# Seven products per pair of d_ff blocks in the gate and up projections of a decoder trunk, with down products between them

## Chip, cores and metric

One NeuronCore of a Trainium2 chip runs the kernel. The metric is device time in microseconds (us); each time is that of one execution, and a kernel's time is the median of its executions. Engines are named as in the profile: PE is TensorE (PEld its weight loads), DVE is VectorE, ACT is ScalarE, POOL is GpSimd, SP issues most of the DMAs. PSUM is the memory that PE accumulates into, in banks; the other engines drain it.

## What is computed

One layer of a decoder for 512 prompt tokens and 8 single-token samples (520 token columns in all), d_model 1024, d_ff 2816, in float32: a mixer of three branches, then the feed-forward sub-layer, then a norm. The change lies in the feed-forward part alone:

```python
def conv_ffn(h, lp, prev):
    a = h @ lp['w_ffn_gate']
    up = h @ lp['w_ffn_up']
    ...
    c = lp['conv_b'] + sum(w[j] * ext[:, j:j + T] for j in range(CONV_W))
    y = (jax.nn.gelu(c) * up) @ lp['w_ffn_down']
    return y, ext[:, T:]
```

`x += conv_ffn(rmsnorm(x))` follows the mixer, and a last `rmsnorm` gives the output.

## The kernel before, in words

**Layout and precision.** Activations stand transposed: 128 channels on the partitions, 520 token columns on the free axis, worked on in two halves of 260 (`NH`, `H`). d_model is 8 blocks of 128 (`KB`), d_ff is 22 (`NFF`). Each operand of a product is kept as two fp32r tiles, a rounded "hi" and the remainder "lo", and `mm3` (L426) issues three matmuls for each pair of 128x128 weight block and 260 columns: hi by hi, hi by lo, lo by hi.

**Weights.** `UNITS` (L56 to L79) is the list of weight units in the order of use; each is up to 8 blocks, 512 KB. `w_load` fetches a unit on SP's queue into a tile `wraw`; `w_split` (L335) makes `whi` (ACT copy) and `wlo` (DVE subtract) of all its 1024 columns. `begin` (L431) and `ahead` (L441) load and split one to two units ahead of use. `product` (L449) issues a unit's matmuls into one of two PSUM tiles `mm` of two banks each, one bank for each token half: 8 blocks x 2 halves x 3 = 48 matmuls. A smaller PSUM tile is called `SD`.

**Order.** The body (L257) is one Python program; DVE, ACT and POOL work that is not tied to a product is kept in generators ("lanes", L230), and `pump` (L394) and `drain` (L408) put their operations between others by a table of modelled costs (`Clock`, L85) at build time. Each engine then runs its own list in order. All operations are recorded by a helper, so the profile gives them line L226.

**Feed-forward part.** For each of 22 d_ff blocks (`for ob in range(NFF)`) a gate unit `fg` and an up unit `fu` are multiplied. The gate product is drained by DVE (times `rs2`), goes through the three-tap convolution (two column copies on POOL, one `Identity` on ACT, two scalar_tensor_tensor on DVE, an add and two copies on POOL), `gelu` on ACT, times `rstd` and times the up product on DVE; ACT's copy and DVE's subtract make the hi and lo tile of hidden block `hid(ob, ·)`. Only then come the down products: for each of 8 output blocks m, 22 hidden blocks in units of 8, 8 and 6, 132 matmuls, one DVE add onto x (`B<-mm,B`). The last output is made in two token halves (`PIECES`, `last`), and `finish` (final norm: two matmuls of `ones` into `SD`, Ln and Exp on ACT, DVE and POOL products, stores) of the first half runs beside the products of the second:

```python
    for c0, n in PIECES:
        for j, _ in enumerate(last(c0, n)):
            if todo and j in (0, 5, 6, 7):
                next(todo, None)
```

Of the kernel before, what the change touches and what calls it, by code (L numbers as in the profile page):

```python
# [15 lines left out]
P = 128  # L16
# [39 lines left out]
def stream_units():  # L56
# [6 lines left out]
    for i in range(NFF):  # L63
        u += [("fg", i), ("fu", i)]
    for i in range(8):
        u += [("dn", (i, 0)), ("dn", (i, 1)), ("dn", (i, 2))]
# [6 lines left out]
def unit_blocks(u):  # L73
    return 6 if u[0] == "dn" and u[1][1] == 2 else 8
# [4 lines left out]
for _u in UNITS:  # L79
    UNIT_OFF.append(_o)  # L80
    _o += P * P * unit_blocks(_u)
N_W = _o


class Clock:  # L85
# [4 lines left out]
    LAT = 0.13  # L90

# [68 lines left out]
    def op(self, eng, name, a, k):  # L160
# [16 lines left out]
        if eng == "pe":  # L177
            if name == "transpose":
                c = 0.9e-3 * a[1].shape[0] + 0.003
            else:  # L180
# [5 lines left out]
                c = 0.417e-3 * max(m, w) + 0.003 if a[1].dtype == F32R else 1.667e-3 * w * (1 if m > 64 else 0.5)  # L186
# [55 lines left out]
EVH = 1.2  # L242
MARG = -0.4
# [13 lines left out]
def body(ctx, tc, I, O):  # L257
# [128 lines left out]
    def ready(l):  # L386

        if l.eng in ("dve", "act"):
            t = 0.0 if l.ready <= clk.t[l.eng] + MARG_Q else l.ready
# [36 lines left out]
    def mm3(ps, wh, wl, xh, xl, first, last):  # L426
        pe.matmul(ps, wh, xh, start=first, stop=False)
        pe.matmul(ps, wh, xl, start=False, stop=False)
        pe.matmul(ps, wl, xh, start=False, stop=last)
# [19 lines left out]
    def product(i, js, xs, kouter=False, mid=None):  # L449
# [3 lines left out]
        ev[0] = EV if n == 8 else EVH  # L453
# [114 lines left out]
    sv = con.tile([P, 528], F32, name="sv")  # L568
    ap = sv[:, 0:288].rearrange("p (n r q) -> p n r q", n=9, r=2)
# [976 lines left out]

    pool.dma_start(O["sk"][:, :127 * 128], I["ckn"][:, 128:])
    pool.dma_start(O["sv"][:, :127 * 128], I["cvn"][:, 128:])
    B_done(2)
    hb = [B(F32R) for _ in range(5)]  # L1550
    hm = M(F32R)

    def hid(ob, part_):
        n = ob if part_ == 0 else 22 + ob
        if n < 40:
            return hb[n // 8][:, (n % 8) * NT:(n % 8 + 1) * NT]
        return hm[:, (n - 40) * NT:(n - 39) * NT]
# [5 lines left out]
    ct = cm[:, 924:1100].rearrange("p (o n) -> p o n", o=NFF)  # L1563
    pool.dma_start(cm[:, 0:352], I["cfc"])
    cw = sm[:, C_CW:C_CW + 66].rearrange("p (o j) -> p o j", j=3)
    dve.tensor_tensor(cpre, cfc[:, :, 0], cw[:, :, 0:1].to_broadcast([P, NFF, 8]), op=OP.mult)
# [4 lines left out]
    cpv = cpre.rearrange("p o (h b) -> p o h b", h=H)  # L1571
    def norm2():
        nonlocal dcol
        dcol = rstd_cols([acc2], (0, 1), NH)

    for ob in range(NFF):
        i = begin("fg")
        if ob == 0:
# [3 lines left out]
            pu = product(i, range(8), blk(yh, yl), kouter=True, mid=lambda: rstd_rows(dcol, rstd))  # L1582
        else:
            ps = product(i, range(8), blk(yh, yl))
        a = T2(524).rearrange("p (h n) -> p h n", h=H)
        pool.memset(a[:, 0, 0:2], 0.0)
# [259 lines left out]
```

## Time and profile before

| | |
|---|---|
| median of 3 executions | 905.75 us (903.94 to 906.66) |
| the profiled execution | 911.76 us, its span 910.0 us |
| granted TensorE clock, mean over the span | 0.984 |
| PE busy | 887.6 us (98%) |
| DVE busy / ACT busy / POOL busy | 518.9 / 345.1 / 131.3 us |
| read from HBM | 91.47 MB |

The span is the time from the first to the last instruction of the one execution that the hardware profiler took. Busy times are of the whole span; a stage that has another mix is read from windows of that stage. Starts are microseconds from the span's start. In a row of the timeline the second number is the length of one instruction (or of the merged run, where "x2" stands at the end); what stands in brackets is the engine's idle time just before and what ended it.

### The profile page before, as it was taken

The page shows a single profiled execution, that of the slowest core. Times are in us where ns is not written, and L with a number is a line of the kernel's source. Part 1 is how long each engine was busy: PE and PEld are TensorE (multiplying, and loading weights), DVE is VectorE, ACT ScalarE, POOL GpSimd, SP SyncE. Part 2 cuts the span into 40 slices and gives each one's busy share as a digit, 9 for nine tenths or more (in the row PEclk, how much of TensorE's full clock was granted, in tenths as well). Part 3 has the DMA queues.
Part 4 walks back from the last instruction along what each step waited for, and adds up shares of the span by engine and source line. Part 5 has one row for each costly group of instructions (what it writes and reads, how often), then busy time and mean ns, then how long its engine had stood idle before and what let it go on. Part 6 is the DMA issues. An engine that isn't in the chain of part 4 may idle for free.

```text
span 910.0 us, 17670 instructions
## 1 busy us (share of the span) xinstructions
PE 887.6 (98%) x7421; PEld 857.4 (94%) x7421; DVE 518.9 (57%) x869; ACT 345.1 (38%) x599; POOL 131.3 (14%) x376
## 2 busy tenths in 40 slices
PE   8999999999899999999999999999999999999995
PEld 8998889998699899799999999999999999999994
DVE  6777768793456696122765655555555555233234
ACT  6375655543434322132333333333333333222231
POOL 7886210002000002100000011111111111000002
PEclk9999999999889999899999999999999999999998
DMA  7433482346324433615223322233222233322212
GB/s 257 166 94 116 129 173 65 118 136 139 77 66 146 137 94 111 141 48 187 93 92 95 92 72 94 93 94 93 93 93 94 93 93 96 106 87 88 86 61 94
DMA packets 38383, 97.83 MB, mean 108 GB/s; under 512 B 12464, under 2 KB 15968, under 8 KB 38032
## 3 DMA queue, kind: packets, MB, share of 16 engines
q1 hardware_dynamic: 35136, 89.53, 32.1%
q0 software_dynamic: 1936, 6.02, 3.1%
q8 instruction: 58, 0.95, 0.4%
q10 hardware_dynamic: 1232, 1.16, 0.4%
q14 instruction: 21, 0.17, 0.1%
HBM read 91.47 MB, written 6.26 MB: 107 GB/s over the span
## 4 chain that ended last, share of the span: by engine, by line
PE 86%; DMA 6%; DVE 4%; ACT 3%; issue 1%; POOL 0%; DVEq 0%; ACTq 0%; POOLq 0%
PE mm L226 75%; PE SD L226 11%; DMA wraw<-in_w 4%; ACT T L226 1%; DVE T L226 1%; DVE B L226 1%; DVE wlo L226 1%; DMA B<-kd 1%; ACT whi L226 1%; POOL B L226 0%; DMA sm<-in_sm 0%; DVE TN L226 0%; ACT B L226 0%; DMA kd<-B 0%; DVEq L1841 0%
## 5 line engine op out<-in xcount | busy, mean ns | idle before, releaser
L226 PE MATMUL mm<-B,whi 128*128 128x260 f32 (+1 forms) x4128 | 762.2, 285 | 5.5 <-DVE B L226 4.4
L226 PEld LDWEIGHTS mm<-B,whi 128*128 128x128 f32 x4128 | 642.1, 189 | 14.2 <-DVE B L226 5.7
L226 PE MATMUL mm<-B,wlo 128*128 128x260 f32 (+1 forms) x2096 | 594.0, 283 | 1.0 <-DVE wlo L226 1.0
L226 PEld LDWEIGHTS mm<-B,wlo 128*128 128x128 f32 x2096 | 397.0, 189 | 1.7 <-DVE wlo L226 1.7
L226 DVE TENSOR_TENSOR wlo<-wraw,whi 128x1024 fp32r<-128x1024 f32 (+2 forms) x157 | 186.5, 1190 | 172.7 <-ACT whi L226 171.9
L226 ACT ACTIVATE whi<-wraw 128x1024 fp32r<-128x1024 f32 (+2 forms) x157 | 160.4, 1023 | 114.7 <-PE mm L226 70.7
L226 DVE SCALAR_TENSOR_TENSOR T<-T,sm,T 128x512 f32<-128x512 f32 x44 | 34.0, 772 | 25.8 <-ACT T L226 25.1
L226 ACT ACTIVATE T<-T,sm 128x520 f32<-128x520 f32 x22 | 18.1, 823 | 79.1 <-POOL T L226 79.1
L226 PE MATMUL SD<-B 128*64 128x72 f32 (+9 forms) x576 | 45.4, 253 | 1.6 <-DMA B<-kd 1.6
L226 DVE TENSOR_TENSOR B<-B 128x256 f32<-128x256 f32 (+11 forms) x78 | 36.3, 474 | 13.4 <-ACT B L226 12.0
L226 PEld LDWEIGHTS SD<-B 128*64 128x64 f32 (+5 forms) x576 | 31.7, 130 | 12.3 <-issue 6.0
L226 ACT ACTIVATE B<-SD 128x256 fp32r<-128x256 f32 (+6 forms) x50 | 19.0, 406 | 60.2 <-PE SD L226 60.0
L226 ACT ACTIVATE B<-T 128x520 fp32r<-128x520 f32 (+1 forms) x32 | 20.4, 638 | 55.0 <-DVE T L226 55.0
L226 POOL COPY T<-T 128x2 f32<-128x2 f32 x22 | 4.1, 184 | 255.1 <-DVE T L226 255.1
L226 DVE TENSOR_TENSOR T<-mm,rstd 128x520 f32<-128x520 f32 x22 | 15.4, 699 | 34.2 <-PE mm L226 31.1
L226 ACT ACTIVATE T<-T 128x520 f32<-128x520 f32 (+3 forms) x27 | 16.3, 606 | 37.6 <-DVE T L226 35.9
L226 ACT ACTIVATE T<-B 128x520 f32<-128x520 f32 (+2 forms) x26 | 15.4, 595 | 38.4 <-DVE B L226 38.4
L226 ACT ACTIVATE B<-B,sm 128x520 fp32r<-128x520 f32 (+1 forms) x23 | 16.7, 727 | 29.6 <-DVE B L226 27.3
L226 ACT ACTIVATE B<-mm 128x520 f32<-128x520 f32 x16 | 9.7, 605 | 46.9 <-PE mm L226 46.9
L226 POOL MEMSET T<- 128x2 f32 (+2 forms) x27 | 4.7, 175 | 152.9 <-DVE B L226 83.6
L226 DVE TENSOR_TENSOR B<-T,B 128x520 fp32r<-128x520 f32 (+1 forms) x30 | 19.1, 638 | 12.9 <-ACT B L226 12.7
L226 ACT ACTIVATE T<-T,TN 128x257 f32<-128x257 f32 (+3 forms) x48 | 21.9, 473 | 11.3 <-DVE TN L226 11.3
(156 smaller groups left out, 663.5 us busy)
## 6 DMA issues: line engine op xcount, KB each, us to landing
wraw<-in_w SPq DMA_DIRECT2D x144, 512.0 KB, 3.5
wraw<-in_w SPq DMA_DIRECT2D x8, 384.0 KB, 3.1
B<-in_xT SPq DMA_DIRECT2D x1, 2080.0 KB, 8.2
B<-kd POOLq DMA_DIRECT2D x16, 128.0 KB, 8.0
B<-in_xT SPq DMA_DIRECT2D x4, 260.0 KB, 5.1
B<-in_xT SPq DMA_DIRECT2D x2, 520.0 KB, 8.1
out_y<-B SPq DMA_DIRECT2D x4, 260.0 KB, 3.2
out_y<-B ACTq DMA_DIRECT2D x4, 260.0 KB, 3.4
```

Of the source, the lines that this page charges most:

```text
L226: return g(*a, **k)
```

## The change

The first six d_ff blocks and all ahead of them stay. Blocks 6 to 21 become eight pairs, p = 3 to 10. A pair's gate (and likewise up) product is a 2 x 2 block product: the two d_ff blocks by the two halves of d_model (4 blocks of 128 each) on the weights' side, A11, A12, A21, A22; the two halves of d_model by the two token halves on the activations' side. It takes seven products (class `Strassen`, table `ORDER`) of sums of blocks instead of eight, each of 4 blocks x 3 = 12 matmuls into one bank of 260 columns. Banks 0 and 1 are those of an `mm` tile, bank 2 is an `SD` tile. Products p0, p2, p4 and p6 accumulate one on top of the other in bank 0, p1 and p3 in bank 2, p5 stands alone in bank 1; after each product the running value is read out (`EVICT`): by an ACT copy after p0, p1, p2 and p6, by a DVE add or subtract onto an SBUF tile after p3, p4 and p5.

The sums on the activations' side are built once into four slots (`build`, as a lane beside the first six blocks, and finished ahead of the first pair). Of the four sums on the weights' side, s1 = A21+A22 and s3 = A21+A11 are made by loading A21 twice and adding 512 KB from HBM onto it with a DMA of POOL's queue that accumulates; s2 = s1+A11 and s4 = s2+A12 by DVE. At each step, `s_step` drains the product before, and sums and splits the weights of the step that comes three later (`D`), 512 columns each, through a ring of six half tiles.

The down products are cut into four groups of hidden blocks (`GROUPS`: the first six blocks, then those of pairs 3 to 5, 6 to 8, and 9 and 10) and stand one by one between the pairs' units in the order of `FF_ORDER`; each adds onto x, so there are 28 such adds of 520 columns where there were 7. In the last group outputs 4 to 7 do their first token halves first; the second halves, 48 matmuls, come last, beside `finish` of the first half.

The build's planner gets other constants for this part (`clk.late`), and the weight array another layout. The diff, cut to its core:

```diff
-    for i in range(NFF):
+    for i in range(6):
         u += [("fg", i), ("fu", i)]
-    for i in range(8):
-        u += [("dn", (i, 0)), ("dn", (i, 1)), ("dn", (i, 2))]
...
+GROUPS = ((0, 1, 2), (3, 4, 5), (6, 7, 8), (9, 10))
+HGROUPS = [[2 * _p + _e for _p in _g for _e in range(2)] for _g in GROUPS]
+HPLACE = {0: (0, 0), 1: (0, 2080), 3: (1, 0), 4: (1, 2080), 5: (2, 0), 6: (2, 2080), 7: (0, 0), 8: (0, 2080),
+          9: (1, 0), 10: (1, 2080)}
+FF_ORDER = ("d0 d0 fg3 d0 fu3 d0 fg4 d0 fu4 d0 fg5 d0 fu5 d0 "
+            "fg6 d1 fu6 d1 d1 fg7 d1 fu7 d1 d1 fg8 d1 fu8 d1 "
+            "fg9 d2 fu9 d2 d2 fg10 d2 fu10 d2 d2 d2 d2 " + "d3 " * 8)
...
+    def mm3(ps, wh, wl, xh, xl, first, last, more=False):
+        k = {"skip_group_check": True} if more else {}
+        pe.matmul(ps, wh, xh, start=first, stop=False, **k)
+        pe.matmul(ps, wh, xl, start=False, stop=False, **k)
+        pe.matmul(ps, wl, xh, start=False, stop=last, **k)
...
+    ysl = [slot() for _ in range(4)]
+    hb = [B(F32R), None, None]
...
+    def build(sl, k):
+        ua, ub, t12 = [hold(make(tmp, [P, 528], F32, "T2", N_T2))[:, :NT] for _ in range(3)]
+        dve.scalar_tensor_tensor(ua, x1[:, k * NT:(k + 1) * NT], gcol(C_GFFN, k), rstd, op0=OP.mult, op1=OP.mult)
+        yield "dve"
+        dve.scalar_tensor_tensor(ub, x1[:, (4 + k) * NT:(5 + k) * NT], gcol(C_GFFN, 4 + k), rstd, op0=OP.mult,
+                                 op1=OP.mult)
+        b11, b12, b21, b22 = ua[:, 0:NH], ua[:, NH:NT], ub[:, 0:NH], ub[:, NH:NT]
+        act.activation(sl.hi[0], b11, AF.Copy)
+        act.activation(sl.hi[1], ub, AF.Copy)
...
+    def y_lane():
+        for k in range(4):
+            yield from build(ysl[k], k)
+            yield "dve", 3
...
+    def places():
+        w = [clk.tile(wrw.tile([P, KB * P], F32, name="wraw", tag="wraw"), "wraw", N_RAW) for _ in range(2)]
+        place[1].update(A11=w[0][:, 0:512], A22=w[0][:, 512:1024], A12=raws[:, 1536:2048], S=w[1])
...
+    COL = {"A21": 0, "A22": 512, "A11": 1024, "A12": 1536}
+    ORDER = (("A11", 0, 0, True), ("s1", 3, 2, True), ("s2", 4, 0, False), ("s4", 2, 2, False), ("s3", 5, 0, False),
+             ("A12", 1, 1, True), ("A22", 6, 0, False))
+    EVICT = ((0, 0, 0, 1.0, 0), (2, 1, 1, -1.0, 0), (0, 0, 1, 1.0, 0), (2, 0, 1, 1.0, 1), (0, 1, 1, -1.0, 1),
+             (1, 0, 0, 1.0, 1), (0, 1, 0, -1.0, 0))
...
+        def load(self, name, s):
+            if name != "S":
+                sp.dma_start(self.A(name), s_dram(self.n, COL[name], 512))
+                return
+            t = place[self.par]["S"]
+            for o in (0, 512):
+                sp.dma_start(t[:, o:o + 512], s_dram(self.n, COL["A21"], 512))
+            later.append((s, lambda: pool.dma_start(t[:, 0:1024], s_dram(self.n, 512, 1024), accum_op=OP.add)))
...
+        def split(self, p, s):
+            name = ORDER[p][0]
+            w = self.A(name)
+            if name == "s2":
+                dve.tensor_tensor(w, w, self.A("A11"), op=OP.add)
+                if self.nxt:
+                    self.nxt.load("A11", s)
+            elif name == "s4":
+                dve.tensor_tensor(w, w, self.A("A12"), op=OP.add)
+            parts_of(s, w, 512)
+            if self.nxt:
+                if name == "s3":
+                    self.nxt.load("S", s + S_LAG)
+                elif name in ("A12", "A22"):
+                    self.nxt.load(name, s)
...
+        def evict(self, p):
+            bank, e, h, sign, add_ = EVICT[p]
+            d = self.dst(e, h)
+            if not add_:
+                act.activation(d, self.acc[bank], AF.Copy, scale=sign)
+            elif sign > 0:
+                dve.tensor_tensor(d, self.acc[bank], d, op=OP.add)
+            else:
+                dve.tensor_tensor(d, d, self.acc[bank], op=OP.subtract)
+            if p == 6:
+                (fg_end if self.kind == "fg" else fu_end)(self.o)
...
+                self.acc = [t[:, 0, :NH], t[:, 1, :NH], SD()[:, :NH]]
...
+        def go(self, p, s):
+            _, f, bank, first = ORDER[p]
+            for k in range(4):
+                w = slice(k * P, (k + 1) * P)
+                xh, xl = ysl[k].get(f)
+                mm3(self.acc[bank], HIW[s][:, w], LOW[s][:, w], xh, xl, first and k == 0, k == 3, not first)
+                spump(0.36 * (3 - k))
...
+    class Down:
+        def __init__(self, n, m, g, halves=(0, 1)):
+            self.n, self.m, self.g, self.halves = n, m, g, halves
+            self.ks = HGROUPS[g]
+            self.q = 4 if len(self.ks) == 4 else 3
+            self.n_steps = len(self.ks) // self.q
+            self.at = [dcount[0] + i for i in range(self.n_steps)]
+            dcount[0] += self.n_steps
...
+        def go(self, p, s, halves=None):
+            n = len(self.ks)
+            for i in range(self.q):
+                k = p * self.q + i
+                w = slice(i * P, (i + 1) * P)
+                for h in halves or self.halves:
+                    c = slice(h * NH, h * NH + NH)
+                    b = self.ks[k]
+                    mm3(self.ps[h], HIW[s][:, w], LOW[s][:, w], hid(b, 0)[:, c], hid(b, 1)[:, c], k == 0, k == n - 1)
...
+            dve.tensor_tensor(hv(x2(m)), self.both, hv(x2(m)), op=OP.add)
+            if self.g == 3:
+                square(m, slice(0, NT))
...
+    def x_add(m, h):
+        x = x2(m, h)
+        dve.tensor_tensor(x, downs[m - 8].ps[h], x, op=OP.add)
+        square(m, slice(h * NH, h * NH + NH))
...
+    def s_step(s):
+        u, p = steps[s]
+        if s:
+            v, q = steps[s - 1]
+            v.evict(q)
+        u.before(p)
+        while later and later[0][0] <= s:
+            later.pop(0)[1]()
+        s_split(s + D)
+        u.go(p, s)
...
+    for ob in range(6):
+        if ob == 4:
+            for name in ("A11", "S", "A12", "A22"):
+                strassens[0].load(name, -1)
+            cu.append(svt[:, 0:512])
+            for _ in range(3):
+                cu.append(hold(make(tmp, [P, 528], F32, "T2", N_T2))[:, 0:512])
+            for j in range(4):
+                dparts[j][0].load(dparts[j][1])
...
+            if ob == 5:
+                for s in range(D):
+                    s_split(s)
...
+    drain([hid_lanes[-q] for q in range(6)])
+    B_done(2)
+    hb[1], hb[2] = B(F32R), B(F32R)
+    places()
+    for name in ("A11", "S", "A12", "A22"):
+        strassens[1].load(name, 3)
+    for s, (u, p) in enumerate(steps):
+        if u is strassens[0] and p == 0:
+            drain([y_build])
+        if isinstance(u, Down) and p == 0 and u.g:
+            w = [hid_lanes[q] for q in GROUPS[u.g] if hid_lanes[q] in lanes]
+            if w:
+                drain(w)
+        s_step(s)
...
+    todo = finish(0, NH, (NH,))
+    next(todo)
+    t = None
+    for i, m in enumerate((4, 5, 6, 7)):
+        d = downs[m - 8]
+        if i % 2 == 0:
+            t = out_tile()
+        d.ps[1] = t[:, i % 2, :NH]
+        d.go(0, d.steps[0], (1,))
+        if m < 7:
+            next(todo, None)
+            x_add(m, 1)
     for _ in todo:
+        pass
+    for _ in finish(NH, NH, (130, 130)):
```

**Order on DVE where up products pass to down products.** Before, `T_8670` holds the last d_ff block's hidden value and `B<-mm,B` is the first down add:

```order
L226 TENSOR_TENSOR T_8666<-mm,rstd 128x2x260
L226 SCALAR_TENSOR_TENSOR T_8670<-T_8666,sm,T_8670 128x2x256 x2
L226 TENSOR_TENSOR T_8670<-T_8670,rstd 128x520
L226 TENSOR_TENSOR wlo<-wraw,whi 128x1024
L226 TENSOR_TENSOR T_8670<-mm,T_8670 128x520
L226 TENSOR_TENSOR M<-T_8670,B 128x520
L226 TENSOR_TENSOR wlo<-wraw,whi 128x768
L226 TENSOR_TENSOR wlo<-wraw,whi 128x1024 x2
L226 TENSOR_TENSOR B<-mm,B 128x520
```

Now the same place comes after block 5, ahead of the first pair (`M` holds loaded weights; `T_6851` to `T_6898` are sums of the fourth slot of activations, `B<-T_...` with two inputs their lo parts; `B<-mm,B` are down adds; the first `M<-M` is s2 of pair 3, the last s4):

```order
L257 SCALAR_TENSOR_TENSOR T_6851<-B,sm,rstd 128x520
L257 TENSOR_TENSOR M<-M 128x512
L257 TENSOR_TENSOR wlo<-M,whi 128x512
L257 SCALAR_TENSOR_TENSOR T_6852<-B,sm,rstd 128x520
L257 TENSOR_TENSOR T_6853<-T_6851 128x260
L257 SCALAR_TENSOR_TENSOR T_6853<-T_6853,T_6852 128x260
L257 TENSOR_TENSOR B<-T_6851,B 128x260
L257 TENSOR_TENSOR B<-T_6852,B 128x520
L257 TENSOR_TENSOR T_6898<-T_6852,T_6851 128x260
L257 SCALAR_TENSOR_TENSOR T_6898<-T_6853,T_6852 128x260
L257 TENSOR_TENSOR B<-T_6853,B 128x520
L257 TENSOR_TENSOR B<-T_6898,B 128x520
L257 TENSOR_TENSOR B<-mm,B 128x520
L257 TENSOR_TENSOR M<-M 128x512
```

Nine operations that begin with block 5's product by `up` stand ahead of these; the fourth slot's build lies between s2 and s4, and a down add too.

**Order on ACT and DVE around a single down unit.** Before, on ACT between two gate products (`T_6150` is a gate value on its way through `Identity` and `gelu`):

```order
L226 ACTIVATE whi<-wraw 128x1024
L226 ACTIVATE T_6150<-T_6146,sm 128x520
L226 ACTIVATE T_6150<-T_6150 128x520
L226 ACTIVATE whi<-wraw 128x1024
L226 ACTIVATE B<-T_6150 128x520
L226 ACTIVATE whi<-wraw 128x1024
```

Now on ACT, from the last read-out of a gate unit (`T_7251<-mm`) past a down unit to the second read-out of bank 0 of the up unit (the second `T_7424<-mm`; `T_7369` is a gate value in the convolution):

```order
L257 ACTIVATE T_7251<-mm 128x260
L257 ACTIVATE whi<-wraw 128x512
L257 ACTIVATE T_7369<-T_7250,sm 128x520
L257 ACTIVATE whi<-wraw 128x512 x2
L257 ACTIVATE T_7424<-mm 128x260
L257 ACTIVATE whi<-wraw 128x512
L257 ACTIVATE T_7425<-SD 128x260
L257 ACTIVATE whi<-M 128x512
L257 ACTIVATE T_7424<-mm 128x260
```

and on DVE over the same stretch (`wraw<-wraw` is s2, `wraw<-wraw,M` is s4, `B<-mm,B` the down add):

```order
L257 TENSOR_TENSOR wlo<-wraw,whi 128x512
L257 SCALAR_TENSOR_TENSOR T_7369<-T_7250,sm,T_7369 128x2x256
L257 TENSOR_TENSOR wraw<-wraw 128x512
L257 TENSOR_TENSOR wlo<-wraw,whi 128x512
L257 SCALAR_TENSOR_TENSOR T_7369<-T_7250,sm,T_7369 128x2x256
L257 TENSOR_TENSOR B<-mm,B 128x520
L257 TENSOR_TENSOR wraw<-wraw,M 128x512
```

The read-out of bank 0 after p0 stands behind the copies of s1, s2 and s4, and s4 on DVE behind the convolution's two operations and the down add.

**Order on DVE at the end.** Before, from the add of the last output's first half to the last product of `finish`:

```order
L226 TENSOR_TENSOR B<-mm,B 128x260
L226 TENSOR_SCALAR T_9909<-SD 128x260
L226 TENSOR_TENSOR T_9910<-T_9908 128x260
L226 SCALAR_TENSOR_TENSOR T_9910<-T_9910,T_9909 128x260
L226 SCALAR_TENSOR_TENSOR T_9908<-T_9910,T_9908 128x260
L226 TENSOR_TENSOR B<-B,T_9908 128x2x260 x2
L226 TENSOR_TENSOR B<-B,T_9908 128x260
L226 SCALAR_TENSOR_TENSOR B<-B,sm,T_9908 128x260
```

Now (`T_9971` is the sum of squares, `T_10143` and `T_10144` belong to `finish`):

```order
L257 TENSOR_TENSOR B<-mm,B 128x260 x2
L257 TENSOR_TENSOR T_9971<-T_9971,T_10164 128x260
L257 TENSOR_SCALAR T_10144<-SD 128x260
L257 TENSOR_TENSOR T_10145<-T_10143 128x260
L257 SCALAR_TENSOR_TENSOR T_10145<-T_10145,T_10144 128x260
L257 SCALAR_TENSOR_TENSOR T_10143<-T_10145,T_10143 128x260
L257 TENSOR_TENSOR B<-mm,B 128x260
L257 TENSOR_TENSOR T_9971<-T_9971,T_10187 128x260
L257 TENSOR_TENSOR B<-B,T_10143 128x2x260 x2
L257 TENSOR_TENSOR B<-B,T_10143 128x260
L257 SCALAR_TENSOR_TENSOR B<-B,sm,T_10143 128x260
L257 TENSOR_TENSOR B<-mm,B 128x260
```

Second-half adds of outputs 4 to 6 now stand among the operations of `finish`, and the last of them behind its large products.

## Rows read from the trace of the kernel before

**Rows 1.** The page, busy time, share of the span and instructions of each engine.
```profile
PE 887.6 (98%) x7421; PEld 857.4 (94%) x7421; DVE 518.9 (57%) x869; ACT 345.1 (38%) x599; POOL 131.3 (14%) x376
```

**Rows 2.** Windows of 30 us: length, then busy time per engine, granted clock, DMA.
```profile
560.00:590.00 30.00, 30.00 (x254) 30.00 (x253) 18.50 (x23) 11.20 (x14) 3.14 (x14) 1.00 0.28 88
830.00:860.00 30.00, 30.00 (x252) 30.00 (x252) 9.54 (x10) 7.39 (x9) 0.00 (x0) 1.00 0.30 97
```

**Rows 3.** The chain of waits: start, length, engine, output tile, line, count.
```profile
527.15 361.94 PE mm L226 x3027
```

**Rows 4.** DVE groups: form, count | busy us, mean ns | idle before, releaser.
```profile
L226 DVE SCALAR_TENSOR_TENSOR T<-T,sm,T 128x512 f32<-128x512 f32 x44 | 34.0, 772 | 25.8 <-ACT T L226 25.1
...
L226 DVE SCALAR_TENSOR_TENSOR T<-B,sm,rstd 128x520 f32<-128x520 f32 x8 | 6.0, 750 | 0.0
...
L226 DVE TENSOR_TENSOR B<-mm,B 128x520 f32<-128x520 f32 x7 | 4.9, 699 | 14.9 <-PE mm L226 14.9
...
L226 DVE TENSOR_TENSOR wlo<-wraw,whi 128x512 fp32r<-128x512 f32 x6 | 4.1, 687 | 1.1 <-ACT whi L226 1.1
...
L226 DVE TENSOR_TENSOR B<-mm,B 128x260 f32<-128x260 f32 x1 | 0.4, 429 | 4.5 <-PE mm L226 4.5
```

**Rows 5.** ACT groups, same columns.
```profile
L226 ACT ACTIVATE T<-T,sm 128x520 f32<-128x520 f32 x22 | 18.1, 823 | 79.1 <-POOL T L226 79.1
...
L226 ACT ACTIVATE whi<-wraw 128x512 fp32r<-128x512 f32 x6 | 3.7, 624 | 1.6 <-DMA wraw<-in_w 1.6
...
L226 ACT ACTIVATE rstd<-SD 128x260 f32<-128x260 f32 x4 | 1.6, 388 | 4.6 <-PE SD L226 4.6
```

**Rows 6.** Timeline of DVE at 201 us: start, length, engine, line, operation.
```profile
201.97 0.69 DVE L226 TENSOR_TENSOR T<-T,TN 128x512 f32<-128x512 f32 x1
202.58 1.22 DVE L226 TENSOR_TENSOR wlo<-wraw,whi 128x1024 fp32r<-128x1024 f32 x1
```

**Rows 7.** Timeline of ACT at 550 us.
```profile
550.08 0.64 ACT L226 ACTIVATE T<-T 128x520 f32<-128x520 f32 x1 [1.71 <-DVE T L226]
550.63 1.05 ACT L226 ACTIVATE whi<-wraw 128x1024 fp32r<-128x1024 f32 x1
```

**Rows 8.** Timeline of all engines at 557 us, the end of a product.
```profile
557.71 0.28 PE L226 MATMUL mm<-B,wlo 128*128 128x260 f32 x1
...
557.82 0.40 PE L226 MATMUL mm<-B,whi 128*128 128x260 f32 x2
...
558.02 0.70 DVE L226 TENSOR_TENSOR T<-mm,rstd 128x520 f32<-128x520 f32 x1 [1.60 <-PE mm L226]
```

**Rows 9.** Who waited for whom: total us, times, longest.
```profile
PE mm L226 <- DVE B L226: 4.4, 4, 3.3
```

**Rows 10.** Windows after that longest wait, columns as in rows 2.
```profile
228.00:234.00 6.00, 3.19 (x20) 2.88 (x20) 3.78 (x6) 2.24 (x6) 0.00 (x0) 0.83 0.79 185
234.00:240.00 6.00, 6.00 (x41) 4.54 (x38) 2.30 (x4) 2.30 (x5) 0.00 (x0) 0.88 0.29 90
```

**Rows 11.** Timeline of PE at the last output, the ones product.
```profile
888.91 0.60 PE L226 MATMUL SD<-T,ones 128*128 128x260 f32 x2
```

**Rows 12.** Timeline of DVE over the last output.
```profile
889.11 0.43 DVE L226 TENSOR_TENSOR B<-mm,B 128x260 f32<-128x260 f32 x1 [4.45 <-PE mm L226]
...
894.50 2.75 DVE L226 TENSOR_TENSOR B<-B,T 128x520 f32<-128x520 f32 x3
897.17 0.47 DVE L226 SCALAR_TENSOR_TENSOR B<-B,sm,T 128x260 f32<-128x260 f32 x1
897.88 0.29 DVE L226 TENSOR_TENSOR B<-mm,B 128x130 f32<-128x130 f32 x1 [0.23 <-PE mm L226]
```

**Rows 13.** DMA issues: queue, count, KB each, median us from issue to landing.
```profile
wraw<-in_w SPq DMA_DIRECT2D x144, 512.0 KB, 3.5
...
B<-in_bm POOLq DMA_DIRECT2D x1, 256.0 KB, 3.1
...
M<-in_cfc POOLq DMA_DIRECT2D x1, 176.0 KB, 12.6
```

## What the change should do to the time

> **What bounds the kernel now.** I read the page's busy times first: PE is busy 98% of the span, DVE 57%, ACT 38% [rows 1]. Then windows inside the two stages that the change touches: in a gate and up stretch PE fills all 30 us and DVE 18.50 (62%), ACT 11.20 (37%); in a down stretch PE again fills all 30, DVE 9.54, ACT 7.39, and the granted clock is 1.00, the upper level of 2.4 GHz, in both [rows 2]. Last the chain of waits: from 527.15 on it is one run of 3027 matmuls in 361.94 us, with nothing between them [rows 3]. So in the whole feed-forward part only the number of matmuls counts, at 361.94/3027 = 0.1196 us each, as long as no other engine becomes late. A product of 12 is 1.43 us, a seven-product unit 10.04, a unit of 48 5.74, a down unit of 36 4.31.
>
> **What goes.** A pair took 4 products of 48 matmuls for gate and up, 192, and takes 2 x 7 x 12 = 168 now: 24 fewer, times 8 pairs = 192 fewer. The down products keep their 1056. 192 x 0.1196 = **-22.96 us**. Everything below is what is given back.
>
> **Prices.** DVE: a split of 512 columns 0.687 us, a convolution tap 0.772, a product with gain and rstd 0.750, a down add of 520 columns 0.699, a 260-column add from PSUM 0.429 [rows 4]. ACT: a split of 512 0.624, `Identity` 0.823, a 260-column read from PSUM 0.388 [rows 5]. In an engine's queue the next operation starts earlier than these lengths end: 0.61 after one of 0.69 on DVE [rows 6], 0.55 after one of 0.64 on ACT [rows 7], so I take 0.08 off inside a queue and leave it on where another engine waits (0.11 with the 0.03 from the end of the last matmul to the read-out's start, [rows 8]). A read-out starts 0.31 after the start of its product's last matmul, which is 0.19 after the next product could start [rows 8]: a matmul's recorded length is pipelined. The weight sums on DVE (two inputs from SBUF, 512 columns) have no row; the nearest are the split and the tap, 0.69 to 0.77, and I take the split's. The 260-column sums for the activations I take at 0.43, the PSUM add's.
>
> **Blocks 0 to 5.** PE's work is unchanged. Beside it DVE must build the four activation slots: two 520-column products (0.75 each), two 520 and one 260 lo parts and so on, 5.7 us a slot in queue time, 22.9 in all. DVE is free (30 - 18.50)/30 of 11.5 us, 4.4 us a block, 24 in five and a half blocks. It just doesn't fit (a convolution cannot wait): 0 to 1 us lost, I take +0.3.
>
> **From block 5 to pair 3.** Let T be the end of block 5's up product. DVE is behind there: laying its queue end to end from the gate product of block 5 (three splits of 384, the rest of the third slot, two taps, the two products, lo), the lo part of hidden block 5 comes at T + 4.2, and the first down unit asks for it at T + 3.6, after 30 of its 36 matmuls. Then one queue runs on: split 384, split 512, down add, split, and the rows shown in the order (the fourth slot, s2, s4), 18 operations, 9.8 us, and some 1.2 of waits for ACT's hi copies that two of them subtract. s4 is summed at T + 15.2. ACT's copy of s4 (0.62) and, behind it in ACT's order, the read-out of p0 (0.34) end at T + 16.2. PE has two down units (8.62) and p0, p1 (2.87) to do, and p2, which accumulates on p0's bank, could start at T + 11.5. So PE waits 4.7 us: **+4.7**. If the planner's lane is displaced by less, 1; if the waits for ACT add up, 7. An idle PE may also cost clock: once before, DVE held PE for 3.3 us [rows 9], and in the 12 us from there the clock was 0.83 and 0.88 of full speed [rows 10], at most (0.17 + 0.12) x 6 = 1.7 us more. I keep this for the range.
>
> **Pairs 3 to 10.** p2, p4 and p6 may not start before the read-out of the product under them. p1, p3 and p5 stand between them on other banks and cover 1.43 us each; the read-out needs 0.19 + 0.39 after its product [rows 5, 8], so it is late only if ACT's queue is. The Trainium skill has a rule against this layout (page "Perfetto Trace Analysis", section "Optimizing Tensor Performance"): independent groups of matmuls should rotate over different PSUM banks, so that reading one out overlaps the next group; four of the seven products here stay on one bank. By the rule, with none of it covered, the sum would get 48 read-outs of 0.70 us, +33.6, where by the rows it gets the wait of a late queue alone. No row of this kernel shows a bank that is accumulated on between read-outs. The tightest place is an up unit after a single down unit. From the end D of the gate unit, at the prices above: read-out 0.19 + 0.34, copy of s1 0.54, `Identity` 0.74, over to DVE 0.11, tap 0.69, s2 0.61, to ACT 0.11, copy of s2 0.54, back 0.11, lo 0.61, tap 0.69, down add 0.62, s4 0.61, to ACT 0.11, copy of s4 0.54, read-out of p0 0.45: D + 7.6. PE gets to p2 at D + 4.31 + 2.87 = 7.18. That is 0.43 us for each of 8 up units; the same for 4 gate units after a single down unit, without the taps, gives about 0.15: **+4.0**. After two down units there are 4.3 us more and nothing is late. Between 0 (an engine's queue is 0.03 quicker at each of fifteen steps) and 12 (1 us in each of 12). As a whole the engines still fit: laid by start to start, DVE has 22.1 us of work in a pair with two down units of 28.7 (77%), ACT 17.3 (60%).
>
> **The end.** From the first `ones` matmul [rows 11] to the first add of the last half the old kernel took 897.88 - 888.91 = 8.97 us and had 66 matmuls to do, so PE set it. Now 48 are left, 18 fewer (2.15 us, counted above already), but DVE sets it: 0.19 to the add, 894.50 - 889.11 = 5.39 for the chain of `finish` up to its large products, some 1.5 for the second-half adds of outputs 4 to 6 and their squares in that queue, 3.1 for the large products (894.50 to the end of that at 897.17, in queue time), 1.2 for two adds behind them: 11.4 [rows 12]. 11.4 - (8.97 - 2.15) = **+4.6**, from 2 (adds in DVE's idle time) to 6.
>
> **The adding transfers.** Sixteen on POOL's queue, 512 KB each, not shown before. The plain load of 512 KB takes 3.5 us; POOL's issues span 3.1 us (256 KB) to 12.6 (176 KB, when others were under way) [rows 13]. From issue to the first use of the sum there are nine steps, one down unit and seven products: 4.31 + 10.03 = 14.3 us. Both ends fit: +0. SP loads A21 twice, in pieces of 256 KB, so its queue gets more and shorter issues; each is asked for a whole unit ahead, and in the windows above DMAs are busy 28% and 30% [rows 2]: +0.
>
> **Sum.** -22.96 + 0.3 + 4.7 + 4.0 + 4.6 = -9.4. The profiled execution, 911.76, would become 902.4; it stood 6.0 above the median of the runs shown, so against 905.75 I predict **896.5**.
>
> **Rivals.**
> *The waits are hidden.* Only the end is paid (and 0 to 1 elsewhere): 905.75 - 22.96 + 4.6 = 887.4, up to 892. For it: DVE is at 77%, and PE falling behind gives it time. Against it: the order puts the read-out of p0 behind three copies. Chance 0.20.
> *The adding transfer is late.* It needs two sources and moves on the queue whose slowest rows are 12.6 us [rows 13]. It decides from 14.3 us on; each us beyond stops PE at s1 of 14 units (the first two have longer). Gain and loss balance at 14.3 + 9.4/14 = 15.0 us; at 16 us it is 14 x 1.7 = +24 and 920. Against it: in this stage DMAs are busy 28% [rows 2] and a plain load lands in 3.5. Chance 0.10. The Trainium skill (page "Collectives: The Full Stack", section "The bandwidth ceiling", on why ReduceScatter is half of AllGather) says that a reducing transfer reads two sources and gets half the rate: doubled by it, the slowest row would give an estimate of 25 us, late by 11 in each unit, the plain load 7 us, which is hidden. No row here shows an adding transfer.
> *The shared bank costs a read-out.* If in each unit one of p2, p4 and p6 waits for its read-out uncovered, 0.31 + 0.39 - 0.11 = 0.59 us [rows 5, 8], beside the waits summed above, that is 16 x 0.59 = +9.4 and the whole gain is gone: 906. It comes about if ACT's and DVE's queues run one operation later than I laid them, since a split or a tap is as long as that. With all three uncovered, 48 x 0.70 = +33.6, it would be far slower, 930; the 1.43 us of the products between speak against that. Chance 0.17, 901 to 908.
>
> That the change does less than it says is excluded: in PE's order 6144 matmuls of 260 columns become 5952.
>
> **How the numbers follow.** Forecast 0.50 (892 to 901), hidden 0.20, bank 0.17, late transfer 0.10, others 0.03. Low end: 905.75 - 22.96 + 1 + 2 = 885.8, so 886. High end: the terms' upper bounds, 1 + 7 + 1.7 + 12 + 6 = 27.7, would all together give 910.5; I stop at 907, which takes in nearly all of the bank rival and leaves out the late transfer. A measurement of this kernel can tell 0.3%, 2.7 us, from no change: faster means below 903.0, slower above 908.5. Faster: the forecast, the hidden case and under half of the bank case, 0.78. Same 0.09. Slower 0.13, the late transfer and the worst of the bank.
>
> **What would show it.** Right: PE 98% busy or a little less; 192 fewer matmuls; DVE without a gap for some 20 us around the end of block 5 and one wait of PE of about 4.7 us in it, released by ACT's read-out of `mm`; waits of PE on ACT of 0.2 to 0.6 in up units after a single down unit, none elsewhere; the adding transfer landing in under 14 us; the first add of the last half 11.4 us after the first `ones` matmul. Wrong: DVE above 85% in windows of the pairs, PE waiting on DVE at every split, or on a DMA at s1; waits at p4 or p6 too, which would be the bank.

## The result: 5% slower, and the profile after

The changed kernel took 951.77 us (median of 4 executions, 947.16 to 955.03) against 906.20 us of the kernel before (4 executions beside it); the ratio is 1.050, with a 95% interval of 1.045 to 1.056. The forecast was 896.5 us, and the range up to 907 does not hold the time.

The page of the changed kernel, busy times and the shares of the chain that ended last:

```profile
PE 886.5 (93%) x7229; PEld 845.7 (89%) x7229; DVE 603.2 (63%) x1099; ACT 406.6 (43%) x797; POOL 151.9 (16%) x392
...
PE 66%; DVE 15%; ACT 9%; DMA 5%; issue 4%; POOL 1%; SPq 0%; DVEq 0%; ACTq 0%; POOLq 0%
```

PE has 192 instructions fewer, as the order said, but its share fell from 98% [rows 1] to 93%. DVE is at 63% over the span; what bounds a stage is read from windows of it. The two windows of [rows 2], which now hold blocks 3 to 5 and pairs with their down products, and one around the start of pair 3 (length, busy time of each engine, clock, DMA):

```profile
560.00:590.00 30.00, 27.41 (x226) 27.05 (x226) 21.96 (x35) 12.65 (x19) 3.81 (x15) 1.00 0.46 128
830.00:860.00 30.00, 28.02 (x228) 27.45 (x228) 20.19 (x34) 13.08 (x27) 4.06 (x11) 1.00 0.43 111
600.00:620.00 20.00, 15.72 (x101) 14.71 (x100) 12.45 (x23) 7.43 (x15) 1.55 (x3) 0.83 0.55 132
```

Where PE was never idle it is idle now, with DVE at 67% to 73%, and in the third window the clock is down. Who waited for whom:

```profile
PE mm L257 <- DVE T L257: 29.4, 36, 1.7
...
PE mm L257 <- DVE B L257: 13.8, 8, 4.1
...
PE mm L257 <- ACT T L257: 4.8, 9, 2.5
```

PE waited for DVE 36 times for 29.4 us where the forecast had waits on ACT. The timeline of PE in the up unit of pair 4, with the first matmul of p5 at 633.51 and of p6 at 635.82:

```profile
630.85 0.28 PE L257 MATMUL SD<-B,wlo 128*128 128x260 f32 x1
...
633.51 0.51 PE L257 MATMUL mm<-B,whi 128*128 128x260 f32 x2 [0.94 <-DVE T L257]
...
634.93 0.28 PE L257 MATMUL mm<-B,wlo 128*128 128x260 f32 x1
...
635.82 0.48 PE L257 MATMUL mm<-B,whi 128*128 128x260 f32 x2 [0.61 <-DVE T L257]
```

and of DVE there:

```profile
633.04 0.41 DVE L257 TENSOR_TENSOR T<-T,mm 128x260 f32<-128x260 f32 x1
...
635.25 0.43 DVE L257 TENSOR_TENSOR T<-mm,T 128x260 f32<-128x260 f32 x1 [0.66 <-PE mm L257]
```

The row at 633.04 reads p4 out of bank 0; p5, which goes to bank 1, starts 0.06 us after its end. The row at 635.25 reads p5 out of bank 1; p6, which accumulates on bank 0, starts 0.14 us after its end. Neither product needs what it waits for: bank 1 was empty, and p4 had been read long before p6. All 16 units of the pairs show the same two waits.

**Where the time went.** I took every stop of PE from the start of one matmul to the start of the next, less 0.1196 us, from the first gate block to the last output. "Slow clock" is the same excess of the matmuls that run at about half the pace behind a stop:

| place | forecast, us | measured, us |
|---|---|---|
| 192 matmuls fewer | -22.96 | -22.96 |
| blocks 0 to 5 | 0.3 | 4.5 |
| from block 5's end to p2 of pair 3; slow clock behind it | 4.7; 0 | 4.9; 2.8 |
| p2 of eight up units (0.41 to 0.47 each); of four gate units | 3.4; 0.6 | 3.6; 0 |
| p5 (1.1 in up units, 0.7 or 1.7 in gate units) and p6 (0.78 each) | 0 | 18.3 and 12.4 |
| last eight outputs: waits; slow clock | 4.6 together | 9.1; 3.6 |

The losses sum to 59.2 us. The span grew by 43.0 (953.0 after 910.0), so 6.8 us more lie elsewhere: most of them in single matmuls that start about 0.1 us late, mostly just behind a stop (5.9 us in all).

### The profile page after: what moved, and what is told of

The parts are those of the page before. It is cut to its first block, busy times and chain, and to the rows that moved or that the text cites. A ratio compares the mean times of both kernels' runs of the same rounds, so it can differ in the third digit from the quotient of the medians.

```text
span 953.0 us, 18057 instructions
## 1 busy us (share of the span) xinstructions
PE 886.5 (93%) x7229; PEld 845.7 (89%) x7229; DVE 603.2 (63%) x1099; ACT 406.6 (43%) x797; POOL 151.9 (16%) x392
## 4 chain that ended last, share of the span: by engine, by line
PE 66%; DVE 15%; ACT 9%; DMA 5%; issue 4%; POOL 1%; SPq 0%; DVEq 0%; ACTq 0%; POOLq 0%
PE mm L257 53%; PE SD L257 13%; DVE T L257 7%; ACT whi L257 5%; DVE wlo L257 4%; DMA wraw<-in_w 4%; ACT T L257 3%; DVE B L257 3%; DVE wraw L257 1%; DMA B<-kd 1%; ACT B L257 1%; POOL B L257 0%; SPq L257 0%; DVE TN L257 0%; DMA kd<-B 0%
## 5 line engine op out<-in xcount | busy, mean ns | idle before, releaser
L257 PE MATMUL mm<-B,whi 128*128 128x260 f32 (+1 forms) x3808 | 712.8, 289 | 48.9 <-DVE T L257 29.4
L257 PEld LDWEIGHTS mm<-B,whi 128*128 128x128 f32 x3808 | 595.4, 191 | 68.1 <-DVE T L257 19.1
L257 PE MATMUL mm<-B,wlo 128*128 128x260 f32 (+1 forms) x1904 | 542.9, 285 | 1.0 <-DVE wlo L257 1.0
L257 DVE TENSOR_TENSOR wlo<-wraw,whi 128x1024 fp32r<-128x1024 f32 (+1 forms) x149 | 153.5, 1031 | 150.9 <-ACT whi L257 146.4
L257 ACT ACTIVATE whi<-wraw 128x1024 fp32r<-128x1024 f32 (+1 forms) x149 | 133.4, 897 | 98.1 <-DMA wraw<-in_w 39.1
L257 DVE TENSOR_TENSOR wlo<-M,whi 128x512 fp32r<-128x512 f32 x64 | 44.3, 691 | 33.3 <-ACT whi L257 30.8
L257 PE MATMUL SD<-B,whi 128*128 128x260 f32 x288 | 54.5, 286 | 0.2 <-DVE B L257 0.2
L257 ACT ACTIVATE whi<-M 128x512 fp32r<-128x512 f32 x64 | 39.7, 626 | 23.2 <-DVE M L257 23.2
L257 PEld LDWEIGHTS SD<-B,whi 128*128 128x128 f32 x288 | 45.3, 192 | 0.4 <-DVE B L257 0.4
L257 PE MATMUL SD<-B,wlo 128*128 128x260 f32 x144 | 41.1, 285 | 0.0
L257 DVE SCALAR_TENSOR_TENSOR T<-T,sm,T 128x512 f32<-128x512 f32 x44 | 33.6, 763 | 2.8 <-ACT T L257 2.6
```

The lines of the kernel that those rows point to most:

```text
L257: return g(*a, **k)
```

## Experiments

Theory A: the two banks of one `mm` tile are waited for as one. Rival B: read-outs and splits are late because DVE's and ACT's queues are full. The program's list of PE instructions, with the semaphores that each waits for, already speaks for A: p5's first matmul waits for DVE, though what it reads is older.

```
L257 MATMUL mm<-B,wlo 128x260
L257 MATMUL mm<-B,whi 128x260 [waits DVE_49]
L257 MATMUL mm<-B,whi 128x260
```

**e1: a tile of its own for p5.**

```diff
-                self.acc = [t[:, 0, :NH], t[:, 1, :NH], SD()[:, :NH]]
+                self.acc = [t[:, 0, :NH], SD()[:, :NH], SD()[:, :NH]]
```

> Edit: the sixth product (p5) of each seven-product unit goes into a PSUM tile of its own instead of the second bank of the tile that p4 and p6 use. Theory A (the two banks of one mm tile are waited for as one: p5 waits for p4's read-out, p6 for p5's): p5's waits of 0.5 to 1.5 us and p6's of 0.61 us go away, except that p6 may wait up to 0.3 us for p4's read-out in the four gate units where that is latest; 31 us less, about 921 us. Rival B (the read-outs and splits are late because DVE's and ACT's queues are full, whichever bank is used): the waits stay or move to the next product, 945 to 952 us.

Measured: 919.39 us, 1.0126 of the kernel before (1.0099 to 1.0153): 32.4 us less than the change, from one line. PE's order is the same; its list now has no wait at p5's first matmul. PE at the first matmuls of p5 and p6 in the same unit (both without a wait), and DVE reading p4 and p5:

```profile
630.21 0.40 PE L257 MATMUL SD<-B,whi 128*128 128x260 f32 x2
...
631.65 0.40 PE L257 MATMUL mm<-B,whi 128*128 128x260 f32 x2
```

```profile
630.84 0.41 DVE L257 TENSOR_TENSOR T<-T,mm 128x260 f32<-128x260 f32 x1
...
632.31 0.41 DVE L257 TENSOR_TENSOR T<-SD,T 128x260 f32<-128x260 f32 x1
```

Here p5 is the row with `SD` (630.21) and p6 the one at 631.65. p4's read-out lies wholly beside p5, and p5's beside p6. The instructions of DVE, ACT and POOL are the changed kernel's, in the same order, so B falls.

**e2: tiles of their own for the half products of the last four outputs.** As e1, and:

```diff
-                t = out_tile() if self.halves == (0, 1) or self.m % 2 == 0 else self.t0
+                t = out_tile()
...
-        if i % 2 == 0:
-            t = out_tile()
-        d.ps[1] = t[:, i % 2, :NH]
+        d.ps[1] = out_tile()[:, 0, :NH]
```

> Edit: as the run before, and every half product of the last four outputs has a PSUM tile of its own instead of sharing one with another output. Theory A: of the three waits of the end (3.8, 0.6 and 4.1 us) the last two go and the first shrinks, and with them the slow clock of the matmuls behind them; 6 to 10 us less than the run before, about 913 us. Rival B (the end is set by DVE's chain of the final norm and its adds): 0 to 2 us less.

Measured: 912.77 us, 1.0058 (1.0039 to 1.0078), 6.6 less than e1. The waits that the changed kernel had at its end:

```profile
920.06 0.77 PE L257 MATMUL mm<-B,whi 128*128 128x260 f32 x2 [3.79 <-DVE B L257]
926.17 0.48 PE L257 MATMUL mm<-B,whi 128*128 128x260 f32 x2 [0.61 <-DVE B L257]
937.55 0.80 PE L257 MATMUL mm<-B,whi 128*128 128x260 f32 x2 [4.14 <-DVE B L257]
```

The last is output 7's second half. It shared a tile with output 6's second half, whose add stood on DVE behind the large products of `finish`, as the order ahead of the prediction shows; it ran from 937.09 on, and PE started behind it. With tiles apart PE's waits over the last eight outputs sum to 6.8 us instead of 9.1, and the granted clock stays at 1.00 from 855 to 902 us. 3.1 of the waits are the last `ones` matmuls standing for DVE's chain of squares; in three others, 0.9, 1.6 and 0.9 us, a half product starts behind DVE's add of an earlier output. That part is DVE's, as B has it.

**f1 and f2: the same cost, alone, in the kernel before.** Only the gate products of blocks 1 to 21 are altered: each token half is read out by itself, the first while the second is multiplied.

```diff
-        hs = [SD()[:, :NH] for h in range(H)] if each else [ps[:, h, :NH] for h in range(H)]
+        hs = [ps[:, h, :NH] for h in range(H)]
...
                     mm3(hs[h], wh, wl, xh, xl, k == 0, k == n - 1)
...
                if each:
                    each(h, hs[h])
...
            product(i, range(8), blk(yh, yl),
                    each=lambda h, p: dve.tensor_tensor(a[:, h, 2:], p, rs2[:, h], op=OP.mult))
```

(The lines with a minus are f2, those with a plus f1; the rest is common to both.)

> Edit: the kernel before, with one thing altered: the gate products of d_ff blocks 1 to 21 are read out half by half, the first token half (first bank of the mm tile) while the second half's matmuls go into the second bank of the same tile. Nothing else moves. Theory A (the banks of one tile are waited for as one): the second half's first matmul waits for the first half's read-out, 0.6 us or more in each of 21 products; 13 to 30 us slower than the kernel before, about 922 us. Rival B (a wait is only for the bank that is read): within 2 us of the kernel before.

> Edit: as f1_halves_one_tile, but the two halves are two PSUM tiles of one bank each; the order of the work is the same. Theory A: no wait, within 2 us of the kernel before, 907 us. Rival B (reading out while PE writes another bank costs time in itself, tile or not): the same waits as in f1.

Measured: f1 943.51 us, 1.0410 (1.0377 to 1.0444); f2 905.56 us, 1.0002 (0.9981 to 1.0022). Same instructions in the same order on every engine, 38 us apart. f1's waits, and one of them with the read-out that it follows:

```profile
PE mm L226 <- DVE T L226: 28.7, 21, 4.3
```

```profile
545.14 0.51 PE L226 MATMUL mm<-B,whi 128*128 128x260 f32 x2 [1.14 <-DVE T L226]
```

```profile
544.66 0.42 DVE L226 TENSOR_TENSOR T<-mm,rstd 128x260 f32<-128x260 f32 x1
```

The second half's first matmul, into an empty bank, starts 0.06 us after the first half's read-out ends. In f2 there is no such wait. A is shown, in a kernel that has nothing else of the change.

The price is above A's 13 to 30 us, and the trace says why. Start to start, 20 of the stops cost 1.38 us each and 0.11 more at the matmul behind; the first, in block 1, costs 4.47, and the 27 matmuls behind it run slow, 2.8 us more. That makes 37.1 us, which is what the stretch from block 0 on grew by (420.2 us in f1, 383.1 in f2).

**e3: no building of the activation slots.** As e2, with one DMA filling each slot (the sums of activations are left out):

```diff
-            yield from build(ysl[k], k)
-            yield "dve", 3
+            pool.dma_start(ysl[k].t[:, 0:3640], yh[:, 0:3640])
+            yield "dve"
```

> Edit: as e2_tail_own_tiles, and the four activation slots are filled by one DMA each instead of being computed by DVE and ACT (leaves out the sums of activations). Theory A (building the slots on DVE delays the convolution of the first six blocks and the start of pair 3): the waits of 4.7 us in the first six blocks and about 5 us ahead of pair 3 go, and the 2 us of slow clock behind the latter; 9 to 12 us less than e2, about 902 us. Rival B (these waits come from the order of the up product and the convolution, which is new as well): the 4.7 us in the first six blocks stay; 5 to 7 us less.

Measured: 905.29 us, 0.9979 (0.9954 to 1.0003), 7.5 less than e2, under the 9 to 12 that A had. The waits that e2 has in the first six blocks and ahead of pair 3 are gone, and so is the slow clock behind them. But there is a new wait in block 1, with ACT's stop for weights ahead of it:

```profile
525.19 0.48 PE L257 MATMUL mm<-B,whi 128*128 128x260 f32 x2 [2.10 <-DVE T L257]
```

```profile
522.12 1.06 ACT L257 ACTIVATE whi<-wraw 128x1024 fp32r<-128x1024 f32 x1 [9.85 <-DMA wraw<-in_w]
```

The edit itself brings it: its four transfers of 1,820 KB took 18.0 us each to landing (median), and the weight loads among them 11.7 where e2's took 3.6. With the slow matmuls behind, that wait costs some 4 us. So the build costs about 11 us; why, this run does not say.

**e4: plain loads.** As e2, without `accum_op=OP.add` (the addition of s1 and s3 is left out).

> Edit: as e2_tail_own_tiles, but the sixteen transfers on POOL's queue load plainly instead of adding (leaves out the addition of s1 and s3). Theory A (they land in 6 us and are needed after 14): within 2 us of e2. Rival (they take bandwidth from the plain loads, on which ACT's copies wait 39 us in all): 3 us or more below e2.

Measured: 912.63 us, 1.0052 (1.0026 to 1.0077): e2's time. The rival falls. The adding transfers of the changed kernel, median us to landing in the last column, landed long before they were needed, and e4's plain ones on the same queue 1.4 to 1.6 us sooner:

```profile
M<-in_w POOLq DMA_DIRECT2D x8, 512.0 KB, 6.1
wraw<-in_w POOLq DMA_DIRECT2D x8, 512.0 KB, 6.4
```

```profile
M<-in_w POOLq DMA_DIRECT2D x8, 512.0 KB, 4.5
wraw<-in_w POOLq DMA_DIRECT2D x8, 512.0 KB, 5.0
```

**e5: less DVE work in the build.** As e2, with the lo parts of the slots made by POOL:

```diff
-        dve.tensor_tensor(sl.lo[0], b11, sl.hi[0].bitcast(F32), op=OP.subtract)
+        for o in range(0, src.shape[1], NH):
+            c = slice(o, o + NH)
+            pool.tensor_tensor(sl.lo[n][:, c], src[:, c], sl.hi[n].bitcast(F32)[:, c], op=OP.subtract)
```

> Edit: as e2_tail_own_tiles, and the lo parts of the activation slots are subtracted by POOL in pieces of 260 columns instead of by DVE (2.2 us of DVE a slot less). Theory A (DVE is full in the first six blocks): the 4.5 us of waits there shrink to under 1.5 and the start of pair 3 comes 2 to 5 us earlier; 905 to 909 us. Rival (POOL's long subtractions delay the convolution's small copies, so the up product is read out as late as before): no change or worse, 912 us or more.

Measured: 912.30 us, 1.0061 (1.0035 to 1.0087). A miss: PE's waits in the first six blocks were 0.8 to 1.7 us as before. But the edit hardly relieved DVE: in the same 65 us of blocks 0 to 5 it was busy 43.8 us instead of 46.2, because its operations ran longer beside POOL's. A split of 384 columns took 1.10 us beside POOL's subtractions (two of them in 2.12) and 0.55 alone:

```profile
586.91 4.98 POOL L257 TENSOR_TENSOR B<-T,B 128x260 fp32r<-128x260 f32 x5
```

```profile
587.99 2.12 DVE L257 TENSOR_TENSOR wlo<-T,whi 128x384 fp32r<-128x384 f32 x2
...
598.95 0.55 DVE L257 TENSOR_TENSOR wlo<-T,whi 128x384 fp32r<-128x384 f32 x1
```

And as the rival has it, the convolution's small additions stood behind POOL's subtractions. So this run does not decide whether DVE is full; e6 does. The timelines of e2 in one of these blocks, DVE first, then ACT, then PE:

```profile
547.26 0.70 DVE L257 TENSOR_TENSOR T<-mm,T 128x520 f32<-128x520 f32 x1
549.61 1.23 DVE L257 TENSOR_TENSOR wlo<-wraw,whi 128x1024 fp32r<-128x1024 f32 x1 [1.65 <-ACT whi L257]
```

```profile
547.99 0.64 ACT L257 ACTIVATE B<-T 128x520 fp32r<-128x520 f32 x1 [1.57 <-DVE T L257]
548.54 1.04 ACT L257 ACTIVATE whi<-wraw 128x1024 fp32r<-128x1024 f32 x1
```

```profile
548.11 0.48 PE L257 MATMUL mm<-B,whi 128*128 128x260 f32 x2 [0.61 <-DVE T L257]
```

ACT stands idle 1.57 us until the product by `up` is done, since its next operation is the copy of that product; only then comes the copy of weights, and DVE stands 1.65 us for that. Two engines that both have idle time (71% and 41% busy) wait for each other in turn, and the next product by `up`, the read-out of an `mm` tile, is late; PE's next product waits for that tile, as the last row shows.

**e6: ACT's weight copies earlier.** As e2, and one number in `product`:

```diff
-                        if h == 0 and k >= 3:
+                        if h == 0 and k >= (0 if clk.late else 3):
```

> Edit: as e2_tail_own_tiles, but in the first six blocks ACT's copy of the next weights is put into its order at a product's first weight block instead of the fourth, ahead of the copy of the hidden value. Theory C (in the first six blocks no engine is full; DVE stands 1.2 to 1.7 us three times a block behind ACT's weight copy, which stands behind the copy of the hidden value, and the up product is read out a block late): DVE's waits shrink, PE's 4.5 us there go down to 2 or less and pair 3 starts as much earlier; 906 to 909 us. Rival (DVE has too much to do there, whatever the order): within 2 us of e2, 911 to 915 us.

Measured: 904.93 us, 0.9965 (0.9937 to 0.9993). Windows over blocks 0 to 5, e2 and then e6:

```profile
527.00:592.00 65.00, 61.17 (x505) 60.47 (x504) 46.21 (x71) 26.93 (x40) 8.88 (x30) 1.00 0.35 104
```

```profile
527.00:592.00 65.00, 64.37 (x539) 64.14 (x538) 53.53 (x85) 30.76 (x47) 11.25 (x30) 1.00 0.42 125
```

In the same 65 us DVE now gets through 85 operations instead of 71, and PE through 539 matmuls instead of 505. PE's waits in the six blocks went from 4.5 to 0.8 us, those ahead of pair 3 from 4.9 to 1.0, and the matmuls behind them kept their pace. Theory C holds: DVE did more in the same time, so it was the order, not the amount. The time is a little below C's 906 to 909 and is e3's, with the slots built.

**e7: whole outputs at the end.** As e6, without halves in the last group: all outputs are multiplied whole, and the final norm of 520 columns follows. One product of that norm also passes from POOL to DVE.

```diff
-            units.append(Down(n, o, g, (0,) if g == 3 and o >= 4 else (0, 1)))
+            units.append(Down(n, o, g, (0, 1)))
...
-    todo = finish(0, NH, (NH,))
...
+    for _ in finish(0, NT, (NH, NH)):
+        pass
```

> Edit: as e6_early_copies, and the last group's outputs are not cut into halves: all eight are done whole, and the final norm of all 520 columns follows the last matmul. Theory (at the end DVE's chain of norm and adds stands between PE's half products; without halves PE ends without waits and one chain of some 15 us is left): 2 to 4 us less than e6. Rival (the norm of the first half was hidden beside products, and now it isn't): 1 to 4 us more than e6.

Measured: 899.83 us, 0.9927 (0.9901 to 0.9953). That is 5.1 less than e6, more than the 2 to 4 of the theory. Over the last eight outputs PE waits once, 0.6 us, instead of 6.8 in all, and 14.6 us follow the last matmul where in e6 it was 11.0. This version, with the change's seven products, is faster than both kernels: 6.6 us (0.7%) under the kernel before, 52 under the change. How much of it the kernel before would gain by the same end was not tried.

## Why the prediction was wrong, point by point

**The step that failed** stands under "Pairs 3 to 10": "p1, p3 and p5 stand between them on other banks and cover 1.43 us each". p1 and p3 are in a tile of their own and did cover; p5 is in another bank of the same tile, and covered nothing. By taking banks as independent it put the waits at p5 and p6 at 0; they cost 30.7 us in the changed kernel, and e1 gave 32.4 back. The change's own list of waits could have told me; I read the order without the semaphores. The profile of before showed it too, at the one place where the two halves of a tile are read out apart, the last output. The read-out of its first half ends at 889.54 [rows 12], and the first matmul of its second half, into the empty bank, waits for DVE and starts 0.06 us later:

```profile
889.60 0.51 PE L226 MATMUL mm<-B,whi 128*128 128x260 f32 x2
```

That is 0.35 us after it could have followed the `ones` matmuls ahead of it. I used these rows for the end alone.

**The rest of that step was right.** I had p2 of an up unit after one down unit 0.43 us late; eight such waits were 0.41 to 0.47. The gate units show none at p2, but in e2 four of 0.36 at p6.

**The shared bank.** The rival had the right kind of wait (a read-out that isn't covered), the wrong place and too small a price, 906 us. Its sign, waits at p6, did show, but for p5's read-out of the other bank. The rule of the Trainium skill that I set against the row (page "Perfetto Trace Analysis", section "Optimizing Tensor Performance") gave +33.6 us, near what was lost in the pairs, but that is a coincidence, and the runs do not bear the reason out: in e1 four of seven products still accumulate on one bank, and that costs 0.4 us here and there; what cost 30 us was a product in a second bank of the same tile.

**Blocks 0 to 5** were taken at +0.3 and cost 4.5. I had counted DVE's free time, which was there (46 of 65 us busy in e2), and not the turns that it takes with ACT. **Ahead of pair 3** the forecast was 4.7 us; 4.9 were measured, the largest part in the wait that I named:

```profile
608.80 0.80 PE L257 MATMUL mm<-B,whi 128*128 128x260 f32 x2 [2.50 <-ACT T L257]
```

2.7 of it are at p2; 1.3 are in the first down unit, at the hi and lo tiles of hidden block 5, and 1.0 in p0 and p1, at the lo parts of the fourth slot. But the cause was partly another than the length of DVE's queue: e6 removed nearly all of it by order alone, so that the sum came out is in part luck. **The slow clock** I had left to the range, at most 1.7; it cost 2.8 behind that wait and 3.6 at the end, where the granted clock was 0.76 in the window from 920 to 940.

**The end.** I had 11.4 us from the first `ones` matmul to the first add of the last half; e2, without the tile wait, shows 900.47 - 889.72 = 10.75. In the changed kernel it was 940.56 - 927.68 = 12.9, with PE's 4.14 us wait in it, and two more waits ahead of it that I did not have.

**The adding transfers** were hidden, as taken: 6.1 and 6.4 us against a cover of 14.3. The doubling that the Trainium skill states (page "Collectives: The Full Stack", section "The bandwidth ceiling"), from which I took an estimate of 7 us for a plain load doubled, is not what these runs show: for the same 512 KB on the same queue adding transfers took 6.4 and 6.5 us in e2 and plain ones 4.5 and 5.0 in e4, 1.3 to 1.4 times as long.

With the tile wait out, e2 came at 912.8, still 16 us above the forecast. Of that, 4.3 lie in the last step of the sum, from the profiled execution to the median: I took 6.0 off, and e2's profiled execution stood only 1.7 above its median. From the last of the twelve 88-column `ones` matmuls of block 0 (at 526.9 us before, 520.0 in f2) to the end of the span it is 383.1 us in both, so what differed between these two executions lies ahead of the change. The forecast for that stretch was 373.7; the changed kernel's profile has 425.6, e2's 385.7, e6's 376.6 and e7's 372.8, one execution each. So e2 is 12.0 above: the first six blocks (4.2), the clock (1.6), p6 (0.9) and the waits ahead of the first `ones` matmul of the end (2.4) make 9.1 of that; the other 2.9, shorter stops among them, stay open.

## What to carry to other kernels

When a PSUM tile spans two banks and one is read out while the other is written, look in the program for a semaphore at the first matmul of the second: give each product that is read out by itself a tile of its own. Before costing a wait by capacity (busy share), lay out both queues of a pair of engines that feed each other; a share of 70% can be a chain with no slack. A saving of matmuls is worth only what the read-outs and splits that come with it leave.

## What the runs showed of the hardware that I had not expected

The stop is in the program, not in the memory: with the same instructions, DVE reading one bank beside PE writing another costs nothing when the two are separate tiles (f2, 905.56 us), and when they are one tile (f1, 943.51 us) PE stands 28.7 us in 21 products.

Some stops cost more than their length. Behind the waits ahead of pair 3 (4.9 us in all, the last of 2.50) nearly thirty matmuls ran at about half the pace, which is the lower of the clock's two levels, 1.2 of 2.4 GHz. A row of the chain, twelve matmuls of p3 in 2.60 us where twelve take 1.43, and a window there, with the granted clock of 0.50 behind the engines' busy times:

```profile
611.77 2.60 PE SD L257 x12
```

```profile
609.00:614.00 5.00, 5.00 (x24) 5.00 (x25) 2.27 (x4) 2.79 (x7) 0.22 (x1) 0.50 0.53 157
```

In e6, where the waits there were 1.0 us, the same matmuls ran at full pace. In f1 the first stop, 4.3 us, had 27 slow matmuls behind it (granted clock 0.50 from 530 to 535 us), and the twenty of about 1.2 us had none (1.00 from 540 to 880). The same holds for the stops of 0.3 to 1.5 us in the pairs of the changed kernel: 1.00 from 620 to 880.

And POOL's work can lengthen DVE's: in e5 a DVE split of 384 columns took 1.10 us beside POOL's subtractions and 0.55 alone.
